# Layer 1's gate behind each tile's norm, and gate chunks of 256 columns

## The chip, the cores and the metric

The kernel is one program on one core of a Trainium2 chip. Five engines work side by side, each through its own queue of instructions in a fixed order: TensorE (PE, matrix products), VectorE (DVE), ScalarE (ACT), GpSimd (POOL) and SyncE (SP), which here only issues DMAs. The metric is the device time of one execution in microseconds (us); the kernel before takes 2372.92 us, the median of three runs from 2371.53 to 2376.02.

## The reference

A decoder trunk of two layers over 1024 tokens of width 1024, all in float32. Layer 0 (retention and mLSTM heads) isn't touched by the change. Layer 1, cut to what matters:

```
u    = rmsnorm(h, norm_pre)
proj = u @ cd_w_in                      # q, k, v, gates, z (1024 wide) and the S5 part
y    = [nsa(...) * silu(z) | s5(...) * silu(sz)] @ cd_w_out       # (1024+512) -> 1024
h    = h + rmsnorm(y, norm_post)
h    = h + sigmoid(h @ pe_gate) * (p @ pe_proj)                   # the gate stage; this is the output
```

`nsa` is attention of 16 heads in 4 groups, with compressed, selected and sliding-window keys.

## The kernel before

Each float32 operand of a product is split into a high and a low part (names end in h and l, or hi and lo), and a product is three products of parts: high by high, high by low, low by high. A product of a 128-token tile with 512 output columns over 1024 inputs is 8 x 3 = 24 PE instructions of 512 columns, over 256 inputs 2 x 3 = 6.

Layer 1 runs in three stages. First come the projections (`nsa_projections`, a generator whose steps are called one by one). Its last part makes z in 16 steps, from weights that `chunk` loads and splits: 2 chunks of 512 columns, 4 load steps each, every one in a buffer of the pool `wsp` (6 of high, 6 of low parts). The same pool then holds the keys and values of a head group, which `group` loads (names kh, kl, vt).

Second comes the attention: 32 units, 4 groups by 8 token tiles, of which one is worked at a time: scores (PE `sc`), softmax (DVE, ACT), scaling of the probabilities `pr` (partly on POOL), their transposes (PE `pt`, split into `pthh` and `pthl`), products with the values (PE `av`). The first PE instruction of a unit's end is `av<-cp,vcT`, by which units are counted here. Beside the units runs a generator, `filler`, that carries other work in small steps; `step` calls it after each part of a unit, so many times as `share` gives for the group. The steps in order: the S5 branch's GLU (PE `gl`), its part of the output product (`fp`, stored to yD), the p products `p @ pe_proj` (stored to ppD), the output products of groups 0, 1 and then 2 (added in yD), and last, for each token tile of group 3 in the order `LAST`, the group's output product, the norm and the residual (lines 1580 to 1605), which leave h in DRAM (hD[2]). The filler has one PSUM buffer (`pF`), four buffers of 512 columns for loaded tiles (tag fin) and four for results (tag fo).

Third, after the attention, `gate_stage` runs the whole gate of layer 1, 8 tiles by 2 halves by 24 products (PE `gp`), with 8 PSUM buffers: it loads h and the stored p products and stores the output. One tile's norm (the last unit's, `late_tile`) is done there too.

The order of the instructions on each engine is made by a scheduler when the program is built, from priorities (`FOFF` sets the filler behind the attention) and buffers; on the chip it is fixed. SP issues its DMAs in that order, and a DMA whose data or buffer isn't ready holds up all behind it.

Of the kernel before, what the change touches and what calls it, by code (L numbers as in the profile page):

```python
# [25 lines left out]
S = 1024  # L26
# [71 lines left out]
def body(tc, A, out, dbg=None):  # L98
# [980 lines left out]
    def nsa_projections(pd):  # L1079
# [47 lines left out]
        for c in range(2):  # L1127
            ck = chunk(W1, [(2608 + 512 * c, 512)])
            for half in range(2):
                for m in range(4):  # L1130
                    ps = pz[0][0].tile([128, 512], FT, name="pj", tag=pz[0][1])
                    proj_col(ps, uT, half, ck, m * 128)
                    zt = pd[0].tile([128, 2, 512], FT, name="zt", tag="st")[:, 0]
                    s.activation(zt, ps, AF.Tanh, scale=0.5)
                    v.scalar_tensor_tensor(zt, zt, 1.0, ps, op0=OP.add, op1=OP.mult)
                    nc.sync.dma_start(zD[4 * c + m, :, half * 512:(half + 1) * 512], zt)
                    yield
# [19 lines left out]
    with ExitStack() as e:  # L1157
# [307 lines left out]
    ext1 = Ext(dict(x=xf), "xxwxwwxw")  # L1465
    with ExitStack() as e:
# [24 lines left out]
        def filler():  # L1491
# [8 lines left out]
            def local_parts(x, nk, eng):  # L1500
                hi = pf.tile([128, 4, 256], FR, name="fhi", tag="fhi")[:, :, :128]
                lo = pf.tile([128, 4, 256], FR, name="flo", tag="flo")[:, :, :128]
# [18 lines left out]
            for l0 in range(0, 8, 2):  # L1521
                hi = pf.tile([128, 4, 256], FR, name="fhi", tag="fhi")
                lo = pf.tile([128, 4, 256], FR, name="flo", tag="flo")
# [22 lines left out]
            for src, w, kt0, nk, dst, add in ((None, W2, 8, 4, yD, False),  # L1546
                                              (A["p"][1, 0], A["pe_proj"][1], 0, 2, ppD, False),
                                              (mixN, W2, 0, 4, yD, True),
                                              (mixN, W2, 4, 2, yD, True)):
                wq = weights(w, kt0, nk)  # L1550
                for i in range(NT):
                    while src is mixN and not all((q, i) in ready for q in ((0, 1) if kt0 == 0 else (2,))):
                        yield
# [14 lines left out]
                    for hf in range(2):  # L1568
                        hs = slice(hf * 512, (hf + 1) * 512)
                        y = ftile("fy", "fo")  # L1570
                        s.activation(y, product(T, wq[hf], nk), AF.Copy, scale=0.25 if src is None else 1.0)
# [6 lines left out]
            wq = wlast[0] = [[load_w(W2, [(hf * 512, 512)], 6, 2)] for hf in range(2)]  # L1578
            for i in LAST[:-NL]:
                while (3, i) not in ready:  # L1580
                    yield
                rows = slice(i * 128, (i + 1) * 128)
                hv = [slice(hf * 512, (hf + 1) * 512) for hf in range(2)]
                x = ready[3, i]
# [3 lines left out]
                T = local_parts(x, 2, g)  # L1588
# [8 lines left out]
                for hf in range(2):  # L1597
# [9 lines left out]
        wlast = [None]  # L1607
# [3 lines left out]
        share = {0: 30, 1: 26, 2: 20, 3: 64}  # L1611
        ready = {}

        def step(gg, n):
            credit[0] += share[gg] * n / 66
            while credit[0] > 0.99:
                credit[0] -= 1
                with tc.issue_after(pace[0].ins), tc.high_priority(offset=FOFF):
                    next(fill, None)

        FOFF = -1000
        for n, (gg, i) in enumerate(units):
            rows = slice(i * 128, (i + 1) * 128)
            zt = n2.tile([128, 2, 128], FT, name="zn", tag="zn", bufs=3)
# [32 lines left out]
            if gg < 3 or i in LAST[-NL:]:  # L1657
# [5 lines left out]
    qx_ = ExitStack()  # L1663
    psB = qx_.enter_context(tc.tile_pool(name="psB2", bufs=5, space=PSUM, reuse_waits="tile"))
    psA = qx_.enter_context(tc.tile_pool(name="psA2", bufs=3, space=PSUM, reuse_waits="tile"))
    with ExitStack() as e:
        pw = e.enter_context(tc.tile_pool(name="pw4", bufs=1, reuse_waits="tile"))

        def late_tile(i, y):

            rows = slice(i * 128, (i + 1) * 128)
            x = pw.tile([128, 2, 128], FT, name="lx", tag="lx")
            nc.sync.dma_start(x, mixN[6:8, :, rows].rearrange("a p k -> p a k"))
            nc.sync.dma_start(y, yD[rows, :])
            x2 = pw.tile([128, D], FT, name="lr", tag="lr")
            gp = pw.tile([128, D], FT, name="lg", tag="lg")
            nc.sync.dma_start(gp, row_ap(A["norm_post"][1], D))
            T = pw.tile([128, 2, 8, 128], FR, name="mhl", tag="thl", bufs=4)[:, :, :2]
            T = T[:, 0], T[:, 1]
            halve(*T, x)  # L1680
            for hf in range(2):
                hs = slice(hf * 512, (hf + 1) * 512)
                ps = psA.tile([128, 512], FT, name="op", tag="psA")
                proj_tok(ps, local(*T), i, wlast[0][hf], 512, nkt=2)
                v.tensor_tensor(y[:, hs], y[:, hs], ps, op=OP.add)
            ms = sm.tile([128, 1], FT, name="ms", tag="ms")
            s.activation(x2, y, AF.Square, accum_out=ms)
            nc.sync.dma_start(x2, hD[1][rows, :])
            r = rstd_of(ms, 1, 1.0 / D, "rs")
            v.scalar_tensor_tensor(y, y, r, gp, op0=OP.mult, op1=OP.mult)  # L1690
            v.tensor_tensor(y, y, x2, op=OP.add)
# [3 lines left out]
    qx_.close()  # L1695
# [33 lines left out]
```

## Time and profile before

The profiled execution took 2375.35 us, with a span of 2373.5 us from the first to the last instruction, so 1.9 us lie outside; it is 2.4 us above the median.

| stretch, us | what runs | PE busy us | DVE | POOL | PE clock |
|---|---|---|---|---|---|
| 1588.29 to 1733.30 | attention group 0, units 2 to 8 | 138.13 | 114.84 | 65.78 | 0.96 |
| 1733.30 to 1908.40 | group 1 | 169.77 | 144.16 | 65.01 | 0.98 |
| 1908.40 to 2087.20 | group 2 | 166.44 | 157.46 | 90.37 | 0.98 |
| 2087.20 to 2237.76 | group 3, units 25 to 31 | 139.25 | 130.95 | 100.81 | 0.95 |
| 2237.76 to 2260.00 | end of unit 32 | 13.26 | 16.13 | 15.24 | 0.92 |
| 2260.00 to 2373.50 | gate stage | 101.80 | 36.02 | 5.19 | 0.97 |

A stretch begins at the first `av` product of a unit. Up to 1500 us PE is busy nearly all the time. Busy time of PE counts a product that runs at half clock twice as long, so a full row isn't PE at its peak.

### The profile page before, as it was taken

To read this page: it belongs to the slowest core of one execution; us is meant where nothing else is said; L and a number is where in the kernel's file an instruction comes from. 1 tells how busy PE (TensorE), PEld (TensorE's weight loads), DVE (VectorE), ACT (ScalarE), POOL (GpSimd) and SP (SyncE) were. 2 spreads that over 40 slices of the span, in tenths; PEclk is the share of its full clock that TensorE was granted. 3 is DMA by queue.
4 is the path that set the end of the run, shared out by engine and by line. 5 is a ranking of instruction groups with operands and counts; after the bars stand their busy time and mean duration, and the time that the engine had idled before them with its cause. 6 is when DMAs were issued, how large, how long until landed. Compare 5 with 4: busy or idle time off the path is not lost.

```text
span 2373.5 us, 34461 instructions
## 1 busy us (share of the span) xinstructions
PE 2279.9 (96%) x11974; PEld 1906.6 (80%) x11974; DVE 1465.5 (62%) x3877; ACT 1069.6 (45%) x2329; POOL 487.5 (21%) x585
## 2 busy tenths in 40 slices
PE   7999999999999999999999999989999989999888
PEld 6878789788888788888888898778888768787667
DVE  6777747755554434343487333377777898898833
ACT  6233323433332432233332332266777777688721
POOL 0122200000000000200000000044544244566710
PEclk9999999999999999999999999989999999999999
DMA  6323312021221745314477423262453333355443
GB/s 159 91 80 104 101 45 72 27 72 35 64 72 36 239 147 203 136 69 134 127 224 234 113 72 116 87 166 67 123 161 117 118 113 101 115 171 162 164 159 112
DMA packets 264647, 279.26 MB, mean 118 GB/s; under 512 B 54384, under 2 KB 196312, under 8 KB 264442
## 3 DMA queue, kind: packets, MB, share of 16 engines
q1 hardware_dynamic: 252618, 243.95, 33.2%
q10 hardware_dynamic: 8240, 24.20, 3.0%
q0 software_dynamic: 3616, 8.92, 1.3%
q8 instruction: 95, 1.56, 0.3%
q14 instruction: 78, 0.64, 0.1%
HBM read 189.84 MB, written 88.42 MB: 117 GB/s over the span
## 4 chain that ended last, share of the span: by engine, by line
PE 82%; DVE 7%; DMA 6%; issue 2%; SPq 2%; ACT 1%; POOL 1%; ACTq 0%; DVEq 0%; POOLq 0%
PE pj L139 40%; PE gp L139 7%; PE op L139 6%; PE fp L139 5%; PE av L139 4%; PE sc L139 4%; PE pt L1485 4%; PE yp L139 2%; PE gl L139 2%; DVE pr L1425 1%; PE trp L214 1%; PE cs L139 1%; PE pp L139 1%; DVE pthl L1477 1%; PE hp L139 1%
## 5 line engine op out<-in xcount | busy, mean ns | idle before, releaser
L139 PE MATMUL pj<-whi,uh 128*128 128x512 f32 (+2 forms) x768 | 278.1, 363 | 4.6 <-ACT whi L163 3.1
L139 PE MATMUL pj<-whi,ul 128*128 128x512 f32 (+2 forms) x768 | 277.4, 361 | 0.0
L139 PE MATMUL pj<-wlo,uh 128*128 128x512 f32 (+2 forms) x768 | 277.3, 361 | 0.0
L1428 ACT ACTIVATE pr<-pr,nm 128x640 f32<-128x640 f32 (+7 forms) x256 | 187.4, 733 | 67.1 <-DVE nm L1425 62.7
L139 PE MATMUL pj<-vh,whi 128*128 128x512 f32 x512 | 204.5, 400 | 0.2 <-ACT vh L218 0.2
L139 PE MATMUL pj<-vh,wlo 128*128 128x512 f32 x512 | 201.9, 394 | 0.0
L139 PE MATMUL pj<-vl,whi 128*128 128x512 f32 x512 | 201.9, 394 | 0.0
L164 DVE SCALAR_TENSOR_TENSOR wlo<-raw,gnp,whi 128x512 fp32r<-128x512 f32 (+3 forms) x248 | 142.5, 611 | 75.4 <-ACT whi L163 74.3
L1477 DVE TENSOR_TENSOR pthl<-pt,pthh 128x512 fp32r<-128x512 f32 x264 | 176.4, 683 | 20.0 <-ACT pthh L1476 16.4
L1476 ACT ACTIVATE pthh<-pt 128x512 fp32r<-128x512 f32 x264 | 149.2, 592 | 49.2 <-PE pt L1485 43.6
L163 ACT ACTIVATE whi<-raw,gnp 128x512 fp32r<-128x512 f32 (+3 forms) x248 | 134.9, 605 | 78.9 <-PE pj L139 36.2
L139 PE MATMUL op<-whi,mhl 128*128 128x512 f32 x520 | 165.1, 395 | 2.5 <-ACT mhl L218 1.7
L139 PEld LDWEIGHTS pj<-whi,uh 128*128 128x128 f32 x768 | 145.0, 189 | 27.6 <-ACT whi L163 3.3
L1485 PE MATMUL pt<-consts,pr 128*128 128x128 f32 x1056 | 162.4, 280 | 4.2 <-DVE pr L1442 2.0
L139 PEld LDWEIGHTS pj<-wlo,uh 128*128 128x128 f32 x768 | 145.7, 190 | 22.3 <-issue 0.7
L139 PEld LDWEIGHTS pj<-whi,ul 128*128 128x128 f32 x768 | 144.8, 189 | 22.1 <-issue 0.2
L1485 PEld LDWEIGHTS pt<-consts,pr 128*128 128x128 f32 x1056 | 133.0, 144 | 28.2 <-issue 4.6
L139 PE MATMUL gp<-whi,mhl 128*128 128x512 f32 x480 | 154.8, 398 | 0.0
L139 PE MATMUL sc<-kh,q 128*128 128x320 f32 (+5 forms) x384 | 142.2, 373 | 11.2 <-DVE nm L1425 10.3
L1442 POOL TENSOR_SCALAR pr<-pr,cf 128x640 f32<-128x640 f32 (+4 forms) x64 | 114.7, 1793 | 150.1 <-DVE cf L1437 71.0
L139 PE MATMUL av<-pthl,vt 128*128 128x512 f32 x264 | 117.5, 445 | 15.8 <-DVE pthl L1477 15.2
L139 PE MATMUL sc<-kl,q 82*128 82x320 f32 (+5 forms) x384 | 127.3, 333 | 0.0
(444 smaller groups left out, 5549.3 us busy)
## 6 DMA issues: line engine op xcount, KB each, us to landing
raw<-in_ab_w_in_dram SPq DMA_DIRECT2D x100, 256.0 KB
raw<-in_cd_w_in_dram SPq DMA_DIRECT2D x30, 512.0 KB
yD<-fy SPq DMA_DIRECT2D x48, 256.0 KB
raw<-in_ab_w_out_dram SPq DMA_DIRECT2D x16, 512.0 KB
raw<-in_pe_gate_dram SPq DMA_DIRECT2D x16, 512.0 KB
qD<-qst SPq DMA_DIRECT2D x16, 512.0 KB
q<-qD SPq DMA_DIRECT2D x32, 256.0 KB
fin<-yD SPq DMA_DIRECT2D x32, 256.0 KB
```

The source lines that it names most:

```text
L139: return t.matmul(o, l, r, start=start, stop=stop, **k)
L163: s.activation(hi[:, k], raw[:, k], AF.Copy, scale=gain(kt0 + k))
L164: v.scalar_tensor_tensor(lo[:, k], raw[:, k], gain(kt0 + k), hi[:, k].bitcast(FT), op0=OP.mult, op1=OP.subtract)
L214: t.transpose(ps[:, k * 128:(k + 1) * 128], x[:, (k4 + k) * 128:(k4 + k + 1) * 128], ident)
L1425: v.tensor_tensor_reduce(pr[:, x:y], ps[:, :y - x], mask[:, x:y], op0=OP.add, op1=OP.min, scale=-1.0, scalar=nm[:, 0:1] if c else 3e38, ac ...
L1428: s.activation(pr[:, :nk], pr[:, :nk], AF.Exp, scale=-1.0, bias=nm[:, c:c + 1], accum_out=sums[:, b, h:h + 1])
L1442: (v if eng == "v" else g).tensor_scalar(P[h][:, :nk], P[h][:, :nk], cf[:, h:h + 1], None, op0=OP.mult)
L1476: s.activation(hi[:dst_shape], ps[:dst_shape], AF.Copy)
L1477: v.tensor_tensor(lo[:dst_shape], ps[:dst_shape], hi[:dst_shape].bitcast(FT), op=OP.subtract)
L1485: t.transpose(ps[:, h * 128:(h + 1) * 128], P[h][:, k * 128:(k + 1) * 128], ident)
```

## The change

Three things are changed. The z weights come in 4 chunks of 256 columns, two load steps each (4 row blocks a step), and the keys of group 0 are asked for one step later (11 for 10). The p products stand behind the output products of groups 0 and 1, and the shares of the four groups are 22, 18, 22 and 76 for 30, 26, 20 and 64. And `gate_stage` is no longer called for layer 1: the filler's last part is, for each of the 8 tiles, `normed` (output product of group 3 and the norm, as before, now with h kept in the two buffers y[0] and y[1]), `turned` (h transposed and split, and both parts stored to a DRAM tile gT) and `gated_out` for the first 512 columns, in the order: norm of a tile, gate of the tile before it, transposes of the tile. The second 512 columns of seven tiles are a generator of their own, `rest`, which loads the transposed parts (gh, gl) and the second half of h (gr) again and uses the attention's buffers; it is run in turn with what is left of the filler after the last unit. The last tile does both halves itself. Where such tiles follow each other, y[0] takes two of the four buffers of tag fo in turn, y[1] one and the gate's `th` one.

```diff
@@ nsa_projections
-        for c in range(2):
-            ck = chunk(W1, [(2608 + 512 * c, 512)])
+        for c in range(4):
+            ck = chunk(W1, [(2608 + 256 * c, 256)])
             for half in range(2):
-                for m in range(4):
+                for m in range(2):
...
-            if n == 10:
+            if n == 11:
                 KV = {0: group(0)}
@@ filler
             for src, w, kt0, nk, dst, add in ((None, W2, 8, 4, yD, False),
+                                              (mixN, W2, 0, 4, yD, True),
                                               (A["p"][1, 0], A["pe_proj"][1], 0, 2, ppD, False),
-                                              (mixN, W2, 0, 4, yD, True),
                                               (mixN, W2, 4, 2, yD, True)):
...
+            gw[0] = [load_w(Wg, [(0, 512)], 2 * k, 2, wp=xf) for k in range(4)]
+            gw[1] = [load_w(Wg, [(512, 512)], 0, 2)]
+            def normed(i):
...
-                    g.tensor_tensor(y[hf], y[hf], x, op=OP.add)
-                    nc.sync.dma_start(hD[2][rows, hv[hf]], y[hf])
+                    (v if done else g).tensor_tensor(y[hf], y[hf], x, op=OP.add)
+                nc.sync.dma_start(hD[2][rows, hv[1]], y[1])
                 yield
+                return y
+            def turned(i, y):
+                hi, lo = (pf.tile([128, 4, 256], FR, name=n, tag=n, bufs=2).rearrange("p a (b k) -> p (a b) k", k=128)
+                          for n in ("fhi", "flo"))
+                for hf in range(2):
+                    ps = pF.tile([128, 512], FT, name="ft", tag="pf")
+                    for k in range(4):
+                        t.transpose(ps[:, k * 128:(k + 1) * 128], y[hf][:, k * 128:(k + 1) * 128], ident)
...
+                    s.activation(hi[:, ks], p3_, AF.Copy)
+                    v.tensor_tensor(lo[:, ks], p3_, hi[:, ks].bitcast(FT), op=OP.subtract)
+                    yield
+                for a, x in enumerate((hi, lo)):
+                    nc.sync.dma_start(gT[i, :, a, :], x.bitcast(FT).rearrange("p k n -> p (k n)"))
...
+            for i in LAST:
...
+                y = yield from truly(normed(i))
+                yield from truly(gate)
+                T = yield from truly(turned(i, y))
+                gate = gated_out(i, 0, T, y[0], pF, "pf")
+            yield from truly(gate)
+            yield from truly(gated_out(i, 1, T, y[1], pF, "pf"))
...
+        def gated_out(i, hf, T, h, pool_, tag):
+            rows, hs = slice(i * 128, (i + 1) * 128), slice(hf * 512, (hf + 1) * 512)
+            ps = pool_.tile([128, 512], FT, name="gp", tag=tag)
+            for k in range(0, 8, 4):
+                proj_tok(ps, local(*(x[:, k:k + 4] for x in T)), 0, gw[hf][k // 2:], 512, nkt=4, start=k == 0, stop=k == 4)
+                yield
+            pp = pf.tile([128, 512], FT, name="pp", tag="fin", bufs=4)
+            nc.sync.dma_start(pp, ppD[rows, hs])
+            th = pf.tile([128, 512], FT, name="th", tag="fo", bufs=4)
+            s.activation(th, ps, AF.Tanh, scale=0.5)
+            v.scalar_tensor_tensor(th, th, 1.0, pp, op0=OP.add, op1=OP.mult)
+            (v if done else g).tensor_tensor(th, th, h, op=OP.add)
+            nc.sync.dma_start(dst_[rows, hs], th)
+        def rest():
+            def fetch(i):
...
+                for a in range(2):
+                    nc.sync.dma_start(T[a].rearrange("p k n -> p (k n)").bitcast(FT), gT[i, :, a, :])
+                nc.sync.dma_start(h, hD[2][i * 128:(i + 1) * 128, 512:])
...
+                yield from gated_out(i, 1, T, h, pS, "sc")
...
-        share = {0: 30, 1: 26, 2: 20, 3: 64}
+        share = {0: 22, 1: 18, 2: 22, 3: 76}
...
-        for _ in fill:
-            pass
+        gw[1] += [load_w(Wg, [(512, 512)], 2 * k, 2) for k in range(1, 4)]
+        done.append(True)
+        gens = [fill, rest()]
+        while gens:
+            for x in list(gens):
+                if x in gens and next(x, gens) is gens:
+                    gens = [y for y in gens if y is not x]
...
-        gate_stage(pw, 1, ext1, hD[2], out if out is not None else dbg["o"], ppD=ppD, order=[7, 6, 5, 0, 1, 2, 4, 3],
-                   late={i: late_tile for i in LAST[-NL:]})
```

What the scheduler makes of it is shown at three places. The first is ACT's queue in the tail, behind the last unit. Before, it holds `mhl<-trp` (the reading of the transposed h), and `th<-gp` (the tanh that ends each half's 24 gate products), freely mixed:

```order
L218 ACTIVATE mhl<-trp 128x512 x2
L963 ACTIVATE th_23734<-gp 128x512
L218 ACTIVATE mhl<-trp 128x512 x2
L963 ACTIVATE th_23765<-gp 128x512
L963 ACTIVATE th_23796<-gp 128x512
L963 ACTIVATE th_23828<-gp 128x512
L218 ACTIVATE mhl<-trp 128x512
L470 ACTIVATE mhl<-lx 128x256
L218 ACTIVATE mhl<-trp 128x512
L963 ACTIVATE th_23927<-gp 128x512
```

In the changed kernel, `fhi<-ft` is the reading of a transposed half (`turned`), `fhi<-zn` the split of a unit's result for its output product, `fin,ms<-fy` the square and sum of the norm, and `fy<-fy,rsb` its scaling (`normed`):

```order
L1657 ACTIVATE th<-gp 128x512
L1616 ACTIVATE fhi<-ft 128x512
L1496 ACTIVATE fhi<-zn 128x2x128
L1616 ACTIVATE fhi<-ft 128x512
L1593 ACTIVATE fin,ms_23240<-fy 128x512 x2
L1601 ACTIVATE fy<-fy,rsb 128x512 x2
L1657 ACTIVATE th<-gp 128x512
L1616 ACTIVATE fhi<-ft 128x512
L1496 ACTIVATE fhi<-zn 128x2x128
L1616 ACTIVATE fhi<-ft 128x512
L1593 ACTIVATE fin,ms_23495<-fy 128x512 x2
L1601 ACTIVATE fy<-fy,rsb 128x512 x2
```

Each tile's five rows come in the same order, with one `th<-gp` (the first 512 columns) to a tile; no gate product of the second 512 columns ends in this piece. PE's queue is alike: 24 `gp`, 8 `ft`, 12 `fp` for a tile. All 384 gate products of the layer stand in PE's queue behind the first `av` product of unit 32, in both kernels.

The second place is SP's queue in the same stretch, with what each row waits for (DMAHWn is the landing of an earlier DMA on one of eight lanes that the program uses in turn, the engines' names are work done there). Before, it loads h and the p products and stores the output:

```order
L967 DMA out_dram<-h_23513 128x1024 [waits DMAHW0_49,DVE_49]
L934 DMA h_23833<-hD_98 128x1024 [waits DMAHW1_49,DMAHW0_49,PE_49]
L961 DMA pp<-ppD 128x512 [waits DMAHW4_49,DVE_49]
L961 DMA pp<-ppD 128x512 [waits DMAHW7_49,DVE_49]
L961 DMA pp<-ppD 128x512 [waits DMAHW2_49,DVE_49]
L967 DMA out_dram<-h_23530 128x1024 [waits DVE_49]
L1674 DMA h_23850<-yD 128x1024 [waits DMAHW6_49,DMAHW5_49,PE_49]
```

In the changed kernel, for one tile: the store of the transposed low part, the loads of both transposed parts, the norm's gain and the residual for both halves, the p products, the store of h's second half, and the next tile's y from yD:

```order
L1620 DMA gT<-flo 128x1024 [waits DMAHW6_49,DVE_49]
L1668 DMA gh<-gT 128x1024 [waits DMAHW7_49,DMAHW5_49]
L1668 DMA gl<-gT 128x1024 [waits DMAHW6_49]
L1599 DMA fin<-in_norm_post_dram 128x512 [waits DMAHW1_49]
L1600 DMA fin<-hD_97 128x512 [waits DMAHW2_49]
L1599 DMA fin<-in_norm_post_dram 128x512 [waits DMAHW3_49,Activation_49]
L1600 DMA fin<-hD_97 128x512 [waits DMAHW4_49,Activation_49]
L1655 DMA pp<-ppD 128x512 [waits DMAHW1_49,Pool_49]
L1604 DMA hD_98<-fy 128x512 [waits Pool_49]
L1587 DMA fy<-yD 128x512 [waits DMAHW7_49,Pool_49]
L1660 DMA out_dram<-th 128x512 [waits DMAHW0_49]
L1587 DMA fy<-yD 128x512 [waits DMAHW6_49,PE_49]
```

The loads of gh and gl have come in ahead of the norm's loads, and each waits for the landing of the gT store that it reads; the second load of fy, into the only buffer of y[1], waits for the store of hD in the row above the first.

The third place is SP's queue where the projections end and the attention begins (`zD<-zt` stores a z step; kh, kl and vt are keys and values). Before:

```order
L1153 DMA vt<-vD 128x8x128 x2
L1146 DMA kh<-kD 64x1024
L1147 DMA kh<-kD 64x1024
L1148 DMA kl<-kD 64x1024
L1149 DMA kl<-akD 18x1024
L1146 DMA kh<-kD 64x1024
L1147 DMA kh<-kD 64x1024
L1148 DMA kl<-kD 64x1024
L1136 DMA zD<-zt 128x512
L1149 DMA kl<-akD 18x1024
```

In the changed kernel the values of group 0 stand ahead of the last five stores of z, and the last store of z stands behind the first loads of the filler:

```order
L1353 DMA q_14182<-qD 128x4x128
L1354 DMA q_14183<-qD 64x4x128
L1355 DMA q_14183<-aqD 18x4x128
L1146 DMA kh<-kD 64x1024
L1147 DMA kh<-kD 64x1024
L1148 DMA kl<-kD 64x1024
L1149 DMA kl<-akD 18x1024
L1153 DMA vt<-vD 128x8x128 x2
L1525 DMA fin<-y5D 128x4x128 x2
L1136 DMA zD<-zt 128x512
```

## Rows read from the trace of the kernel before

**Rows 1.** the page: PE's busy time, and the chain that ended last by engine.

```profile
PE 2279.9 (96%) x11974; PEld 1906.6 (80%) x11974; DVE 1465.5 (62%) x3877; ACT 1069.6 (45%) x2329; POOL 487.5 (21%) x585
PE 82%; DVE 7%; DMA 6%; issue 2%; SPq 2%; ACT 1%; POOL 1%; ACTq 0%; DVEq 0%; POOLq 0%
```

**Rows 2.** by stretch: busy us (instructions) of PE, PEld, DVE, ACT, POOL; clock, DMA share, GB/s.

```profile
1733.30:1908.40 175.10, 169.77 (x954) 143.97 (x953) 144.16 (x457) 136.04 (x299) 65.01 (x69) 0.98 0.38 122
1908.40:2087.20 178.80, 166.44 (x902) 134.56 (x900) 157.46 (x449) 132.97 (x271) 90.37 (x88) 0.98 0.34 107
2087.20:2237.76 150.56, 139.25 (x749) 113.57 (x747) 130.95 (x387) 123.31 (x282) 100.81 (x99) 0.95 0.54 172
2260.00:2373.50 113.50, 101.80 (x460) 82.19 (x460) 36.02 (x54) 19.28 (x35) 5.19 (x5) 0.97 0.37 132
```

**Rows 3.** timeline of PE: first product of units 28 and 32.

```profile
2167.68 0.39 PE L139 MATMUL av<-cp,vcT 128*128 128x512 f32 x1
2237.76 0.40 PE L139 MATMUL av<-cp,vcT 128*128 128x512 f32 x1
```

**Rows 4.** chain of waits, 2180 to the end: start us, us, what.

```profile
2199.94 5.07 DMA hD<-fy
2205.03 2.11 DMA fy<-yD
2218.36 3.54 DMA fy<-yD
2230.68 5.37 DMA hD<-fy
2236.07 2.58 DMA fy<-yD
2254.89 4.58 DMA fin<-in_norm_post_dram
2266.17 6.36 DMA h<-hD
2345.23 22.44 PE gp L139 x96
```

**Rows 5.** instructions of a normed tile, by line: duration ns min/median/max.

```profile
L1592 DVE TENSOR_TENSOR fy<-fy,fp x14: 667/682/690, 2169.4 to 2254.0; 128x512 f32<-128x512 f32 x14
L1593 ACT ACTIVATE fin<-fy x14: 619/626/644, 2170.1 to 2254.8; 128x512 f32<-128x512 f32 x14
L1593 ACT ACTIVATION_READ_ACCUMULATOR fin<-fy x14: 186/193/210, 2170.6 to 2255.3; 128x1 f32 x14
L226 POOL TENSOR_TENSOR rsb<-rsa,mhalf x8: 548/566/731, 2176.3 to 2328.9; 128x1 f32<-128x1 f32 x8
L1601 ACT ACTIVATE fy<-fy,rsb x14: 707/710/728, 2178.7 to 2257.9; 128x512 f32<-128x512 f32 x14
L1602 POOL TENSOR_TENSOR fy<-fy,fin x14: 1260/1288/1301, 2179.5 to 2262.2; 128x512 f32<-128x512 f32 x14
```

**Rows 6.** page, costliest groups: reading a 128x512 PSUM tile into two parts.

```profile
L1477 DVE TENSOR_TENSOR pthl<-pt,pthh 128x512 fp32r<-128x512 f32 x264 | 176.4, 683 | 20.0 <-ACT pthh L1476 16.4
L1476 ACT ACTIVATE pthh<-pt 128x512 fp32r<-128x512 f32 x264 | 149.2, 592 | 49.2 <-PE pt L1485 43.6
```

**Rows 7.** timeline of the last microseconds: ACT and SP.

```profile
2367.69 0.60 ACT L963 ACTIVATE th<-gp 128x512 f32<-128x512 f32 x1 [5.01 <-PE gp L139]
2369.77 0.34 SPq L967 DMA_DIRECT2D out_dram<-h  x1
```

**Rows 8.** timeline around the first attention unit: PE, SP, DVE.

```profile
1537.75 1.36 PE L1485 MATMUL pt<-consts,pr 128*128 128x128 f32 x11
1554.15 0.35 SPq L1136 DMA_DIRECT2D zD<-zt  x1
1561.16 1.89 DVE L1477 TENSOR_TENSOR pthl<-pt,pthh 128x512 fp32r<-128x512 f32 x3 [2.41 <-DMA vt<-vD]
1561.91 0.80 PE L139 MATMUL av<-pthl,vt 128*128 128x512 f32 x1 [5.80 <-DVE pthl L1477]
```

More of the change, by code (lines that the diff above doesn't have):

```diff
@@ L1464, in body @@
     W2 = A["cd_w_out"][0]
-    ext1 = Ext(dict(x=xf), "xxwxwwxw")
     with ExitStack() as e:
@@ L1577, in filler @@
                         yield
[L1578 to L1581, printed above, removed]
+            wq = [[load_w(W2, [(hf * 512, 512)], 6, 2)] for hf in range(2)]
+            gw[0] = [load_w(Wg, [(0, 512)], 2 * k, 2, wp=xf) for k in range(4)]
+            gw[1] = [load_w(Wg, [(512, 512)], 0, 2)]
+            def normed(i):
                 rows = slice(i * 128, (i + 1) * 128)
                 hv = [slice(hf * 512, (hf + 1) * 512) for hf in range(2)]
-                x = ready[3, i]
                 y = [ftile("fy", "fo") for _ in range(2)]
@@ new lines, in filler @@
+            gate = iter(())
+            for i in LAST:
+                while (3, i) not in ready:
+                    if next(gate, False) is False:
+                        yield False
+                    else:
+                        yield True
+                y = yield from truly(normed(i))
[4 more added lines that the diff above has]
+            yield from truly(gated_out(i, 1, T, y[1], pF, "pf"))
@@ new lines, in truly @@
+        def truly(gen):
+            while True:
+                try:
+                    next(gen)
+                except StopIteration as e:
+                    return e.value
+                yield True
+        def gated_out(i, hf, T, h, pool_, tag):
[11 more added lines that the diff above has]
+            nc.sync.dma_start(dst_[rows, hs], th)
@@ new lines, in rest @@
+        def rest():
+            def fetch(i):
+                T = [np_.tile([128, 1024], FR, name="g" + x, tag="pr0", bufs=5).rearrange("p (k n) -> p k n", k=8) for x in "hl"]
+                h = np_.tile([128, 640], FT, name="gr", tag="pr1", bufs=4)[:, :512]
+                for a in range(2):
+                    nc.sync.dma_start(T[a].rearrange("p k n -> p (k n)").bitcast(FT), gT[i, :, a, :])
+                nc.sync.dma_start(h, hD[2][i * 128:(i + 1) * 128, 512:])
+                return T, h
+            X = {}
+            for n, i in enumerate(LAST[:-1]):
+                for m in (n, n + 1):
+                    if m not in X and m < len(LAST) - 1 and LAST[m] in stored:
+                        X[m] = fetch(LAST[m])
+                while n not in X:
+                    yield
+                    if i in stored:
+                        X[n] = fetch(i)
+                T, h = X[n]
+                yield from gated_out(i, 1, T, h, pS, "sc")
@@ L1608, in body @@
+        Wg, dst_ = A["pe_gate"][1], out if out is not None else dbg["o"]
+        gT = dram.tile([8, 128, 2, S], FT, name="gT")
+        gw, done, stored = {}, [], set()
         fill = filler()
         credit = [0.0]
-        share = {0: 30, 1: 26, 2: 20, 3: 64}
+        share = {0: 22, 1: 18, 2: 22, 3: 76}
         ready = {}
@@ L1616, in step @@
             while credit[0] > 0.99:
+                with tc.issue_after(pace[0].ins), tc.high_priority(offset=FOFF):
+                    work = next(fill, None)
+                if work is False:
+                    break
                 credit[0] -= 1
-                with tc.issue_after(pace[0].ins), tc.high_priority(offset=FOFF):
-                    next(fill, None)
         FOFF = -1000
```

53 lines of the change are left out of this document (14 added, 39 removed).

## The prediction

> **What bounds the kernel now.** I read the page first: PE is busy for 96% of the span and holds 82% of the chain that ended last [rows 1], so time can only come from where PE waits or runs at half clock. The stretches say where. In group 1 PE is busy for 169.77 of 175.10 us, so filler work taken out there is time gained. In group 3 it is 139.25 of 150.56 at a mean clock of 0.95, with DVE at 130.95 and POOL at 100.81: something else ends waits there [rows 2]. Units 28 to 31 take 2237.76 - 2167.68 = 70.1 us [rows 3], while PE's queue holds for them 66 filler products, 44 products with values, 70 of scores (at most 512 columns each), 84 transposes and 16 short ones. At 22.44 / 96 = 0.234 us for a product of 512 columns [rows 4], 1.36 / 11 = 0.12 us for a transpose [rows 8] and an estimated 0.2 for a score, that is 25.7 + 14 + 10 + 2 = 52 us. So about 18 us are waits or half clock, and the chain shows what kind: between 2200 and 2240 it runs through the filler's own DMAs, h stored, then the next y loaded, 7.2 to 8 us for each such pair [rows 4]. Last, the tail. From the start of unit 32 to the end is 2373.5 - 2237.76 = 135.7 us, and the gate stage keeps PE busy for 101.80 of its 113.50 us [rows 2].
>
> **The change part by part.** The z chunks: PE's products stay the same, the load steps too (8), but 32 splits of 256 columns replace 16 of 512 on ACT and on DVE. A half-width split costs no more than a whole one, so 16 extra at no more than 0.6 to 0.7 us [rows 6] are at most 11 us on each engine, beside a stretch of some 100 us that PE fills. I put it at nothing; were PE to wait for weights there, it is those 11 us. Where the attention begins, PE waits 5.8 us until 1561.91, for a DVE instruction that was let go at 1561.16; its buffer is free only when the last z store has landed, and that store left SP at 1554.15 [rows 8]. In the new queue the values of group 0 go five z stores earlier, and SP isn't held by them before the last store; but kh, kl and vt of group 1 and two loads of y5D still stand ahead. Gain between 0 and 7 us; I take 3, the middle.
>
> The filler: behind unit 32's start PE's queue holds 72 fp products for 24 before (12 of them named op), so units 1 to 31 hold 48 fewer, 11.2 us of PE. By groups it is +10, -34, -24 and 0. The loss is in groups 1 and 2, where PE is busy for 97% and 93%, so nearly all of it should show: 9 us, with 3 to 11 as bounds, less where a unit is then bound by DVE. In group 3 norm tiles leave (five tiles' output products and norms, or more, now lie behind unit 32) and p products come, which need no POOL and end in one ACT read. Of the 18 us of waits in units 28 to 31 I take 5 back; the bounds are 0 and 12. Together the last unit begins 17 us earlier (3 to 30).
>
> The tail. The gate isn't hidden in the attention: all 384 of its products stand behind unit 32's start, as before. Behind that point PE has 72 + 384 + 21 = 477 products and 72 transposes, 111.6 + 8.6 = 120 us at full clock, against 429 and 92, 100.4 + 11 = 111 us, that took 135.7. So PE has 9 us more to do, and what decides is how long it waits. Before, eight PSUM buffers and loads made well ahead kept it fed. Now the order for tiles 5, 0, 1, 2 is 24 gp, 8 ft, 12 fp, again and again, with no product of the second half between, as ACT's queue shows (one tanh to a tile); and all three kinds use the one buffer of pF. One cycle, from the DVE add that ends a tile's output product to the next tile's, goes so:
> - square and its sum 0.63 + 0.19, two tiny DVE operations (estimate 0.3), power 0.57, scaling 0.71: 2.4 us; then POOL, two products and two sums of 1.29 each: 5.15 [rows 5]. h is ready after 7.6 us.
> - its second half is stored, and the next y[1] loads into the same buffer only when that has landed: 5.07 to 5.37 us from store to load, then 2.11 to 3.54 until y is there [rows 4], and 0.68 for the add [rows 5]. That closes the cycle at 15.5 to 17.2 us.
> - PE's own work in it is 36 products and 8 transposes, 8.4 + 1.0 = 9.4 us, with two reads of 0.59 + 0.68 [rows 6] behind the transposes. These fit beside the chain. PE waits 6 us or more in each.
> - The norm's gain and residual are late too. SP sends them behind gh and gl, and these wait until the gT store has landed. A 512 KB store that left at 2369.77 with nothing beside it took the 3.7 us to the end of the span [rows 7]. The y load leaves 3.3 us before the new cycle begins and the stores right behind it, so gh and gl leave at about +1 and the gain at +2 to +3; with 1 MB ahead of it (512 KB took 6.36 us, a gain of 256 KB 4.58 [rows 4]) it lands at +5.5 to +8.5, where POOL wants it at +2.4. That adds 3 to 6 us: 19 to 23.
>
> I take 20 us a cycle. To the end of tile 5's output product there are 83 products and 24 transposes, 22.3 us, and some reads: 25. Four cycles are 80. Behind them stand 207 products and 16 transposes (48.4 + 1.9), now with second halves between, and the last tile's reads: 56. The end, tanh to landed store, was 5.8 [rows 7] and is 5 with half the store. 25 + 80 + 56 + 5 = 166, 30 more than 135.7. With cycles of 16 us it is 150, 14 more; with 25, 186, 50 more.
>
> Sum: -17 + 30 = +13. The profiled execution's own 2375.35 us (span plus 1.9) becomes 2388; the median of the runs lies 2.4 lower, so I forecast 2386.
>
> On what a DMA takes: the rows show 5.07 and 5.37 us for a store of 256 KB and 2.11 to 3.54 for a load [rows 4]. The Trainium skill (DMA: Bandwidth & Descriptors, section Anatomy of one DMA) gives about 2.0 us fixed plus the bytes at 436 GB/s, an estimate of 2.6 us for either. Loads agree with that, stores don't. By it a cycle would be near 14 us and the time near the first rival's.
>
> **The rivals.** First, faster: the queue is calm once the attention has ended, every DMA lands in the 2.11 us of the shortest row [rows 4] and the gain is in time. Then a cycle is 7.6 + 2.1 + 0.4 + 2.1 + 0.7 = 13 us, the tail 25 + 52 + 56 + 5 = 138, and the time 2372.9 - 17 + 2.3 = 2358. For it: the attention's loads are gone. Against: a cycle moves 4.5 MB (gT out and back 2, y, gain and residual 1.5, p, h and output 1), in 13 us 346 GB/s, twice the 172 of group 3 [rows 2]. The point is the cycle: below 15.5 us the kernel is faster, from 15.5 to 17.9 it can't be told from no change, above it is slower.
>
> Second, no change: cycles of 16 to 17 us, that is no lateness of the gain but slow stores. 25 + 66 + 56 + 5 = 152, +16, and 2372.
>
> Third, much slower: the 4.5 MB crowd the queue so that stores and gain land later still, 25 us a cycle, and groups 1 and 2 give back little because DVE (157.46 of 178.80 in group 2 [rows 2]) takes over: -10 + 50, 2413. Half of it, no gain in the attention (-3) with cycles of 20, is 2400.
>
> **How the numbers follow.** Forecast, slower by cycles of 18 to 22 us: 0.50, with its own range 2378 to 2400. Much slower: 0.18. No change: 0.13. Faster: 0.19. About 0.2%, 4.7 us, can be told from no change here. So slower 0.68, same 0.13, faster 0.19. The range that leaves a tenth on either side is 2362 to 2412: it takes in half of the first rival's case and most of the third's.
>
> **What would show it.** In the profile after, unit 32's first value product should stand near 2221 us (2208 to 2235), and about 166 us should follow it. In that stretch PE should be busy for about 0.75 of the time, with four cycles in which 24 gp, 8 ft and 12 fp take 18 to 22 us, and a clock below 0.95 there. PE's waits should be for DVE's add of the output product, which waits for fy<-yD, and for POOL's sums behind fin<-in_norm_post. The second halves should run together at the end at 0.234 us a product. PE should wait less than 5.8 us where the attention begins. The forecast is wrong if the cycles take under 16 us, if the second halves' products fill them, or if the attention ends more than 30 us earlier.

## The result, and the profile after

The changed kernel is slower: 2429.24 us (median of four runs, 2425.1 to 2432.67), a ratio of 1.0232 to the kernel before, interval 1.0207 to 1.0257, or +55 us. The forecast was 2386, with 2412 as the upper end: right in sign, and too small by more than its range allowed. The kernel before took between 2365.6 and 2374.5 us (medians) beside the change and the runs below, so kernels are compared by their ratios.

By its page PE is busy for 2298.5 us, for 2279.9 before [rows 1], in a span that is 50 us longer. The stretches say where the time is. Unit 32 begins at 2222.57, 15.2 us earlier than [rows 3]. These are groups 1, 2 and 3 and then everything from unit 32 on, which I call the tail (columns as in [rows 2]):

```profile
1723.62:1885.89 162.27, 158.57 (x894) 132.44 (x892) 138.98 (x427) 126.17 (x271) 73.05 (x75) 0.99 0.39 119
1885.89:2067.59 181.70, 168.15 (x902) 136.31 (x900) 157.43 (x474) 134.81 (x280) 79.04 (x81) 0.95 0.31 97
2067.59:2222.57 154.98, 140.20 (x761) 114.16 (x760) 128.50 (x374) 121.98 (x273) 82.49 (x77) 0.95 0.45 147
2222.57:2423.30 200.73, 146.11 (x550) 108.75 (x548) 51.96 (x83) 43.80 (x86) 45.40 (x43) 0.83 0.55 182
```

The tail of the kernel before, the same view:

```profile
2237.76:2373.50 135.74, 115.06 (x522) 92.02 (x520) 52.14 (x80) 33.84 (x65) 20.43 (x17) 0.96 0.39 138
```

The tail is 65.0 us longer. PE is idle in it for 200.73 - 146.11 = 54.6 us (before 20.7) and busy for 31 us more; 9 of those are the added work that the prediction counted (120 against 111 us at full clock), the other 22 are, as an estimate, more products at the lower clock level (0.83 of the full clock for 0.96). The prediction divided the tail into three parts: up to tile 5's output product, four tile cycles, the rest. It gave them 25, 80 and 61 us; they took 26.5, 89.5 and 84.7:

```profile
2222.57:2249.06 26.49, 23.54 (x107) 18.37 (x106) 10.29 (x17) 10.39 (x20) 8.37 (x8) 0.96 0.59 185
2249.06:2338.59 89.53, 65.64 (x222) 47.07 (x221) 17.44 (x29) 20.11 (x41) 30.12 (x28) 0.77 0.57 191
2338.59:2423.30 84.71, 56.93 (x224) 43.31 (x222) 24.22 (x37) 13.30 (x25) 6.90 (x7) 0.85 0.52 171
```

In a cycle one link of the forecast's chain is the main one: the gT store has to land before SP sends the loads behind it, the norm's gain among them, and only then can POOL start (start, us, what):

```profile
2266.80 5.49 DMA gT<-flo
2272.30 0.32 SPq L1668
...
2272.67 6.46 DMA fin<-in_norm_post_dram
...
2279.27 1.26 POOL fy L1602
...
2281.87 2.49 POOL fy L1603 x2
...
2284.99 1.26 POOL th L1659
2286.26 0.69 POOL flo L1497
...
2288.81 5.60 DMA gT<-flo
```

From one gT store to the next that is 2288.81 - 2266.80 = 22.0 us. The other link of the forecast, the store of h and the load of y behind it, isn't on this chain: in the four cycles DVE's adds of an output product waited for PE's product (3.0 to 3.1 us in most) or not at all, never for y. PE has a chain of its own of the same length through its one buffer: the first gate product of a tile starts at 2274.06, of the next at 2295.41. In between PE waits for the readings of pF and once for POOL's sum (in brackets), and its products follow each other at 0.43 us, but for the second 12 gate products, which take 0.23:

```profile
2274.06 0.79 PE L139 MATMUL gp<-whi,fhi 128*128 128x512 f32 x1 [0.78 <-DVE fy L1592]
...
2275.07 0.63 PE L139 MATMUL gp<-whi,flo 128*128 128x512 f32 x1
2275.50 0.63 PE L139 MATMUL gp<-whi,fhi 128*128 128x512 f32 x1
...
2279.46 0.40 PE L139 MATMUL gp<-wlo,fhi 128*128 128x512 f32 x1
2279.69 0.39 PE L139 MATMUL gp<-whi,flo 128*128 128x512 f32 x1
...
2283.19 0.66 PE L1614 MATMUL ft<-consts,fy 128*128 128x128 f32 x4 [1.06 <-POOL fy L1603]
2285.66 0.87 PE L1614 MATMUL ft<-consts,fy 128*128 128x128 f32 x4 [1.81 <-DVE flo L1617]
2287.94 0.80 PE L139 MATMUL fp<-whi,fhi 128*128 128x512 f32 x1 [1.41 <-DVE flo L1617]
...
2291.70 0.79 PE L139 MATMUL fp<-whi,fhi 128*128 128x512 f32 x1 [0.83 <-DVE fy L1592]
...
2295.41 0.79 PE L139 MATMUL gp<-whi,fhi 128*128 128x512 f32 x1 [0.78 <-DVE fy L1592]
```

The rest is where the forecast had no waits. The two longest of PE there:

```profile
2354.19 0.80 PE L139 MATMUL gp<-whi,gh 128*128 128x512 f32 x1 [9.08 <-ACT th L1657]
...
2398.27 1.12 PE L1614 MATMUL ft<-consts,fy 128*128 128x128 f32 x4 [7.42 <-ACT th L1657]
```

And the chain up to the first of them:

```profile
2339.47 4.99 DMA fin<-in_norm_post_dram
2344.60 1.28 POOL fy L1602
2345.89 3.38 DMA pp<-ppD
2349.29 0.70 DVE th L1658
...
2350.74 2.72 DMA out_dram<-th
2353.54 0.61 ACT th L1657
2354.19 7.39 PE gp L139 x24
```

PE waits for a tanh to read a full PSUM buffer; the tanh for the store of the half before it, since th has one buffer; that half for its p products, whose load needs one of the four buffers fin, which the norm's gain and residual fill too: SP sends it at 2345.89, when POOL's product with the gain has ended. In the whole tail ACT stands idle for 31.3 us, six times, until such a store has landed.

### The profile page after: what moved, and what is told of

It is laid out like the page before. It is cut to its first block, busy times and chain, and to the rows that moved or that the text cites. A ratio compares the mean times of both kernels' runs of the same rounds, so it can differ in the third digit from the quotient of the medians.

```text
span 2423.3 us, 34597 instructions
## 1 busy us (share of the span) xinstructions
PE 2298.5 (95%) x11974; PEld 1912.2 (79%) x11974; DVE 1466.9 (61%) x3890; ACT 1076.1 (44%) x2349; POOL 494.6 (20%) x591
## 5 line engine op out<-in xcount | busy, mean ns | idle before, releaser
L164 DVE SCALAR_TENSOR_TENSOR wlo<-raw,gnp,whi 128x256 fp32r<-128x256 f32 (+3 forms) x264 | 144.8, 587 | 75.8 <-ACT whi L163 74.9
L1476 DVE TENSOR_TENSOR pthl<-pt,pthh 128x512 fp32r<-128x512 f32 x264 | 176.1, 683 | 20.1 <-ACT pthh L1475 17.3
L163 ACT ACTIVATE whi<-raw,gnp 128x256 fp32r<-128x256 f32 (+3 forms) x264 | 138.0, 586 | 79.7 <-PE pj L139 38.3
L139 PE MATMUL av<-pthh,vt 128*128 128x512 f32 x264 | 111.3, 422 | 7.9 <-ACT pthh L1475 7.9
```

The costliest lines, as they stand in the source:

```text
L139: return t.matmul(o, l, r, start=start, stop=stop, **k)
L163: s.activation(hi[:, k], raw[:, k], AF.Copy, scale=gain(kt0 + k))
L164: v.scalar_tensor_tensor(lo[:, k], raw[:, k], gain(kt0 + k), hi[:, k].bitcast(FT), op0=OP.mult, op1=OP.subtract)
L1476: v.tensor_tensor(lo[:dst_shape], ps[:dst_shape], hi[:dst_shape].bitcast(FT), op=OP.subtract)
```

## The experiments

In the table, "unit 32" and "tail" are from each kernel's profiled run (us), the ratio is to the kernel before on the same chip.

| run | unit 32 at | tail | median us | ratio (95%) |
|---|---|---|---|---|
| e1 z256 | 2220.7 | 135.2 | 2360.76 | 0.9964 (0.9949 to 0.998) |
| e2 z256_porder | 2235.1 | 163.4 | 2397.18 | 1.0117 (1.0082 to 1.0151) |
| e3 th_buffers | 2219.5 | 197.1 | 2421.37 | 1.0224 (1.0196 to 1.0252) |
| e4 gain_kept | 2222.0 | 194.3 | 2427.14 | 1.0247 (1.021 to 1.0283) |
| e5 tail_psum | 2223.7 | 175.9 | 2400.5 | 1.0139 (1.0114 to 1.0165) |
| e6 p_first | 2235.7 | 176.0 | 2417.18 | 1.0229 (1.0194 to 1.0263) |
| e7 porder_old_shares | 2247.4 | 132.0 | 2385.58 | 1.0087 (1.0055 to 1.0119) |
| e8 p_first_psum_th | 2241.2 | 158.1 | 2400.17 | 1.0141 (1.0121 to 1.0162) |
| e9 hold | 2220.1 | 205.0 | 2430.2 | 1.0251 (1.0228 to 1.0273) |
| e10 hold_busy | 2223.4 | 208.8 | 2432.6 | 1.0263 (1.0239 to 1.0288) |
| e11 hold_psum_th | 2219.8 | 175.9 | 2399.23 | 1.0117 (1.0087 to 1.0147) |
| e12 hold_gain | 2218.2 | 159.8 | 2383.81 | 1.006 (1.0038 to 1.0082) |
| e13 direct | 2227.6 | 149.9 | 2373.27 | 1.002 (1.0007 to 1.0034) |
| e14 direct_gain | 2216.8 | 143.7 | 2365.15 | 0.9988 (0.9971 to 1.0006) |
| e15 direct_p_first | 2234.6 | 132.8 | 2373.86 | 1.0012 (0.9995 to 1.0029) |

**Which part of the change costs what: e1, e2, e7, e6.** e1 is the kernel before with the first hunk of the diff alone.

> The kernel before with the z chunks of 256 columns (and the keys of group 0 asked for a step later) alone. The changed kernel's first attention unit ended 8.5 us earlier by then (second unit's first value product at 1579.82 for 1588.29). If the chunks did that: the second unit at about 1580 and a time 6 to 9 us below the kernel before, 2365. Rival: the lighter filler of group 0 (share 22 for 30) did it: the second unit at about 1587, time within 3 us of before.

It is faster, ratio 0.9964, -8.5 us. The wait of 5.80 us [rows 8] is gone, but PE now waits 7.51 us for the step before it, where it waited 3.25 before (in the changed kernel, second piece, 7.76). The second unit starts at 1580.47 for 1588.29:

```profile
1556.75 0.80 PE L139 MATMUL av<-pthh,vt 128*128 128x512 f32 x1 [7.51 <-ACT pthh L1476]
...
1580.47 0.39 PE L139 MATMUL av<-cp,vcT 128*128 128x512 f32 x1
```

```profile
1558.26 0.80 PE L139 MATMUL av<-pthh,vt 128*128 128x512 f32 x1 [7.76 <-ACT pthh L1475]
```

Unit 32 comes 17.0 us earlier, with all other parts of the change left out; in this run groups 0 and 3 were 5.6 and 3.0 us shorter too. By the ratio half of that, 8.5 us, is gained; the rest lies between the two profiled runs. e2 adds the new order of the p products and the new shares, e7 the order alone, both on the kernel with the old gate stage. Both also take over the changed kernel's `step`, in which a call that finds the filler blocked no longer uses up credit, so that the order is never tested without it.

> The kernel before with the z chunks, the p products behind the output products of groups 0 and 1, and the shares 22, 18, 22, 76; its own gate stage stays. If what the change gained in the attention is a gain by itself: the last unit's first value product some 10 to 20 us earlier than 2237.76, and a time of 2355 to 2366. Rival: filler moved out of groups 1 and 2 comes back in group 3 and behind it, so that only the z chunks' 8 us are left or less: 2364 to 2375.

> The kernel before with the z chunks and the p products moved, but with its own shares 30, 26, 20, 64. If it was the shares that cost the 36 us of e2 (less filler in groups 0 to 2, so more norm tiles late): 2358 to 2370. If it was the order of the products: 2390 to 2400.

e2 came out above both of its ranges, e7 (by its ratio 2394) in its second. Against e1, e2 is 1.5% slower and e7 1.2%, so most of the loss is the order's. In e7 the tail is no longer than that of e1 and group 1 is the main loser (first row): 198 us for 173.4, with x1032 on PE for x957. By the code the filler, blocked until the outputs of groups 0 and 1 are there, keeps its credit and then works in a burst; group 2 has those products less and got only 6 us shorter, and group 3 8 us longer. With the smaller shares (e2) most of the loss comes out behind unit 32 instead (second row, x564 for x522 in e1): some 30 more products of output products stand there, with their norms, ahead of the gate stage.

```profile
1719.93:1917.89 197.96, 190.49 (x1032) 160.95 (x1032) 145.62 (x439) 138.38 (x294) 93.07 (x90) 0.98 0.42 131
```

```profile
2235.07:2398.50 163.43, 129.39 (x564) 101.62 (x562) 58.56 (x97) 44.59 (x87) 37.56 (x32) 0.91 0.45 148
```

e6 goes the other way: the changed kernel with the p products first and the old shares.

```diff
+                                              (A["p"][1, 0], A["pe_proj"][1], 0, 2, ppD, False),
                                               (mixN, W2, 0, 4, yD, True),
-                                              (A["p"][1, 0], A["pe_proj"][1], 0, 2, ppD, False),
...
-        share = {0: 22, 1: 18, 2: 22, 3: 76}
+        share = {0: 30, 1: 26, 2: 20, 3: 64}
```

> The changed kernel with the p products in front of the output products again and the shares 30, 26, 20, 64, as before the change; z chunks and gate in the filler stay. The p order alone cost some 36 us beside the z chunks in the kernel with the old gate stage (e2 against e1). If it costs as much here (norm tiles pushed behind the last unit): 2385 to 2400, that is what the gate in the filler costs alone, with the last unit at about 2221 and a tail of 165 to 180. If the tail's length is the gate cycles' alone, whatever stands ahead: 2415 to 2430.

Its ratio is 1.0229, that of the change, as in the second expectation: unit 32 is 13 us later, the tail 25 us shorter, in the profile; in the runs' ratio nothing. So beside the new gate the order and the shares cost nothing that the runs can tell, and the price of the gate in the filler is e6 against e1: 1.0229 / 0.9964, +2.7% or 63 us. The parts don't add up: beside the new order and shares the gate costs 1.0232 / 1.0117, some 27 us, and the order with its shares costs 36 beside the old gate (e2 against e1).

**Single causes in the tail: e3, e4, e5, e8.** e3 gives th three buffers, e4 loads the gain once, e5 spreads the tail over the attention's free PSUM buffers:

```diff
-            th = pf.tile([128, 512], FT, name="th", tag="fo", bufs=4)
+            th = (n2.tile([128, 512], FR, name="th", tag="pthh", bufs=3).bitcast(FT) if done else
+                  pf.tile([128, 512], FT, name="th", tag="fo", bufs=4))
```

```diff
...
-                gate = gated_out(i, 0, T, y[0], pF, "pf")
+                gate = gated_out(i, 0, T, y[0], *((pT, "pt") if done else (pF, "pf")))
...
```

> The changed kernel, but the gate's result th behind the attention takes three buffers of its own (those of the probabilities' high parts, free by then), which also leaves all four result buffers to the two halves of the normed tile. Theory A (the tail is long since a tanh waits until the store of the half before it has landed, and PE behind the tanh): the 31 us that ACT stood idle for these landings go, the waits of 9.08 and 7.42 us on PE go, and the second halves' products run within the tile cycles: 2400 to 2410 for 2429. Theory B (the tail is long since SP sends the norm's gain and residual behind the loads of gh and gl, which wait for the gT store): the cycles stay at 21 us, 2420 to 2428.

> The changed kernel, but the norm's gain is loaded once behind the attention, into a buffer of the mask that is free by then, for 2 loads of 256 KB in each tile. Theory B (the gain, queued behind gh, gl and the gT store, comes late to POOL): four cycles shrink from 21 us by 3 to 5, 2409 to 2418. Theory A (result buffers): the residual still stands in the same place of SP's queue and the end of the tail is as it was, 2422 to 2430.

> The changed kernel, but behind the attention the gate's first halves and the transposes take the attention's free PSUM buffers (three of pT) and the second half of an output product that of pV, for the one buffer of pF. Theory C (a tile's cycle of 21.3 us is PE's own chain through one PSUM buffer, each step waiting for the reading of the one before, and that at half the clock since PE has gaps): the waits of PE for th, flo and fy at 0.8 to 1.8 us each go, the cycles fall to 15 to 17 us and the granted clock in the tail rises above 0.81: 2400 to 2412 for 2429. Theory D (the cycle is DVE, POOL and the y load): the cycles stay at 20 to 21 us, PE waits for POOL's or DVE's fy instead: 2422 to 2430.

e3 and e4 changed the ratio by no more than its interval. e5 took some 22 us off (1.0139 for 1.0232). All three had a flaw that I saw only then: "if done" is decided when the code of a tile is written out, and the tiles of the first cycles are written out while units are still left. So e4 is no test of theory B (e12 is): of the 12 loads of the gain in the changed kernel's tail 8 are still there, those of the cycles.

In e3 the edit did reach the second halves. The waits of 9.08 and 7.42 us for a tanh are gone and some second halves stand in the cycles, as theory A has it, but the tail is only 3.6 us shorter: PE now waits 5.28 and 6.52 us for DVE, whose reading of pF (flo) stands in its queue behind the halves' own products with p:

```profile
2359.35 1.12 PE L1614 MATMUL ft<-consts,fy 128*128 128x128 f32 x4 [5.28 <-DVE flo L1617]
...
2394.57 1.12 PE L1614 MATMUL ft<-consts,fy 128*128 128x128 f32 x4 [6.52 <-DVE flo L1617]
```

In e5 the first cycles keep the one buffer and are much as they were: between gate starts 20.2, 23.9 and 20.3 us for 21.4, 21.2 and 22.8. Its gain is in the part behind them, the third of the prediction: from the fifth gate start to the end it takes 60.9 us, in the changed kernel 83.9 (the rows of both, e5 first), and no wait of PE for a tanh above 0.8 us is left.

```profile
2338.75:2399.60 60.85, 51.45 (x221) 40.71 (x219) 22.97 (x34) 11.54 (x22) 7.11 (x6) 0.95 0.67 226
```

```profile
2339.37:2423.30 83.93, 56.23 (x220) 43.09 (x220) 23.54 (x36) 13.28 (x25) 6.90 (x7) 0.85 0.52 172
```

e8 is e6 with the edits of e3 and e5.

> The changed kernel with p products first and the old shares, with the tail's PSUM buffers of pT and pV and with three th buffers. If p order, PSUM buffer and th buffer add up (36, about 20 and 8 us): 2360 to 2375, level with the kernel before. If the norm chain and its DMAs bound the tail whatever the buffers: 2385 to 2400.

1.0141, 0.9% below e6: as much as the PSUM buffers alone brought in e5. The parts don't add up.

**All tiles alike: e9 to e11.** e9 writes six of the tiles out behind the attention, in turn with the second halves:

```diff
-                while (3, i) not in ready:
+                while (3, i) not in ready or i in LAST[2:] and not done:
```

> The changed kernel, but the filler takes up only the first two tiles of group 3 while units are left; the other six are written out behind the attention, in turn with the second halves. Nothing else is changed, and PE's queue then has 24 products of a second half in every tile cycle, where the changed kernel has four cycles without. Theory E (the second halves stand at the end because the tiles were written out ahead of them, and the cycles without them run at half clock with gaps): cycles of 60 products and 8 transposes, 15 us at full clock, take 18 to 20 us, nothing is left for the end, the tail falls from 200.7 to 150 to 165 us and the granted clock rises above 0.9: 2380 to 2395 for 2429. Theory F (each cycle is the chain of y load, norm and PSUM reads, whatever PE has beside it): cycles of 24 to 28 us, 2410 to 2430.

Theory E falls. Now each cycle has 60 products, but takes 25 to 27 us, after a first of 32. The idle time of PE in this tail, by what it waited for (us in total, times, longest):

```profile
PE ft L1614 <- DVE flo L1617: 10.7, 7, 2.9
PE ft L1614 <- ACT th L1657: 10.1, 5, 4.1
PE gp L139 <- DMA gh<-gT: 8.9, 4, 3.3
PE gp L139 <- DMA gl<-gT: 7.2, 4, 2.3
PE fp L139 <- DVE flo L1617: 7.1, 5, 1.4
```

No wait is the main one. The second half of a tile, moved into the cycles, now waits for its own round trip through gT.

> e9 with products added that nobody reads: 6 behind the transposes of a half, 3 behind a half's output product, 18 to a tile in six tiles, some 108 products or 25 us at full clock, put where PE waits for pF to be read. If PE's gaps cost through the clock: the clock in the tail rises, and the time is at most 5 us above e9 or below it. If the clock is no matter (PE is bound by its work or by the chain): 15 to 25 us above e9.

```profile
2223.43:2432.20 208.77, 163.92 (x658) 126.83 (x656) 58.90 (x94) 43.86 (x86) 33.50 (x32) 0.89 0.51 174
```

108 products that nobody reads (x658 for x550) cost 3.7 us in the tail and nothing that the runs can tell, at a clock of 0.89 for 0.86. PE's work isn't what bounds the cycles. Whether the clock alone costs anything can't be told from this: PE was busy for 20 us more and little else moved.

> e9 with the tail's PSUM buffers of pT and pV and three th buffers, now for all six tiles (in e5 and e3 the first four cycles, written out before, kept the one buffer). If the waits for the one pF buffer (0.8 to 1.8 us, six to a cycle) are what is left: the cycles fall to 16 us and the tail to 135 to 145, 2365 to 2378. If the norm's loads and stores bound it: no more than 5 us below e9.

1.0117: 31 us below e9, between its two expectations, and still 22 to 23 us a cycle. PE's waits for pF are gone; the chain of DMAs is left, here from one gT store to the next:

```profile
2336.29 3.42 DMA gT<-fhi
...
2341.09 6.03 DMA fin<-in_norm_post_dram
...
2347.25 1.27 POOL fy L1603
...
2349.29 1.12 PE ft L1616 x4
2350.41 7.07 PE gp L139 x22
...
2359.12 3.24 DMA gT<-fhi
```

**The DMA chain: e12 to e15.** e12 is e11 with the gain loaded once; e13 is e11 with the second halves made from the parts where they lie; e14 is both; e15 is e14 with the p products first. From the diff of e13:

```diff
...
-                nc.sync.dma_start(hD[2][rows, hv[1]], y[1])
+                if i in LAST[:2]:
+                    nc.sync.dma_start(hD[2][rows, hv[1]], y[1])
...
+                if i in LAST[2:]:
+                    gate = both(gate, gated_out(i, 1, T, y[1], pT, "pt"))
...
```

> e11 with the norm's gain loaded once behind the attention. In e11 a tile's cycle is still 22 us, and the chain of waits runs through the gT store (3.0 to 3.4 us), then the gain load sent behind it (5.7 to 6.0), POOL's product, the transposes, 22 gate products and the next gT store. If the gain's place in SP's queue holds the cycle: it falls by 4 to 6 us in five cycles, 2370 to 2380 for 2399. If the residual's load, which stands in the same place, takes over: within 4 us of e11.

> e11 without the round trip through DRAM for the last six tiles: their second halves take the transposed parts and h from the buffers in which they were made, so that gT and h aren't stored and gh, gl, gr not loaded (2.5 MB less for a tile); the gain is loaded for each tile as before. If the round trip (the store's landing and SP's queue behind it) holds the cycle: 16 to 17 us, PE's own 14 and a little, the tail 135 to 145: 2360 to 2370. If the order of norm, turn and gate holds it in itself: 20 us and more, 2385 to 2400.

> e13 and e12 together: no round trip and the gain loaded once, three PSUM buffers, three th buffers. Six tiles of 60 products and 8 transposes are 15 us each at full clock. If DMA was all that held the cycles: the tail is that of e1 (135), and the time that of e1 or a few us above (2360 to 2368), since units 2 to 31 take as long. If it stays above 2375 the norm's chain through ACT, POOL and DVE is what is left.

All three went the way of their first theories, e12 and e13 not quite so far. In e11 the gain's place in SP's queue is worth 13 us (1.006 for 1.0117), the round trip 23 (1.002), both 31 (0.9988). In e14's tail PE has the 550 instructions of the changed kernel's, and is busy for 123.63 us for 146.11, the clock at 0.95 for 0.83; the second half of a tile is transposed at 2294.83, 2311.06, 2326.98 and 2343.05, a cycle of 16 us with 60 products in it (first row and the two pieces of the timeline). The second row is e1's tail: PE is idle for 20.1 us in both, so what e14's tail is longer by, 8.5 us, is PE's added work, not waiting.

```profile
2216.82:2360.50 143.68, 123.63 (x550) 97.52 (x548) 61.85 (x94) 43.22 (x86) 33.82 (x32) 0.95 0.41 136
```

```profile
2220.74:2355.90 135.16, 115.05 (x522) 91.91 (x520) 51.89 (x80) 33.54 (x65) 20.12 (x17) 0.95 0.40 139
```

```profile
2294.83 0.63 PE L1620 MATMUL ft<-consts,fy 128*128 128x128 f32 x4 [0.57 <-DVE fy L1607]
...
2311.06 0.63 PE L1620 MATMUL ft<-consts,fy 128*128 128x128 f32 x4 [0.58 <-DVE fy L1607]
```

> e14 with the p products in front and the shares 30, 26, 20, 64 again. In e6 that moved the last unit 13 us later and made the tail 25 us shorter, at cycles of 21 us. If with short cycles a tile costs in the tail what it costs in the attention, nothing is gained: 2362 to 2372. If the tail still has waits that the attention would hide: 2350 to 2360, below e1.

1.0012: unit 32 is 18 us later, the tail 11 us shorter, and nothing is gained, nearer to the first expectation. No form of the gate in the filler came below e1, which is the version that beats both kernels.

## Why the prediction was wrong

- **The sign** was right, and the mechanism in part: the gate's work stays behind the attention, and there it runs in cycles in which the gain comes late behind the gT store. Of the 43 us that the forecast missed, 34.7 lie in the tail.
- **The attention**: unit 32 was to begin near 2221 and began at 2222.57, by errors that cancel: that is luck. The z chunks were put at -3, with 7 as their most: the second unit began 8.5 us earlier in the changed kernel, and alone (e1) the chunks gave 8.5 us in the time. The wait where the attention begins, to be less than 5.8 us, was 7.76. Groups 1 and 2 were to give 9 and gave 12.8 - 2.9 = 9.9. Group 3 was to give 5 and took 4.4: taking norms out and putting p products in didn't shorten its waits.
- **The cycle** was put at 20 us, from 19 to 23. The two that hold nothing else took 21.35 and 21.15 (gate start to gate start, up to 2316.56), the four together, with 22 and 24 products of a second half in the first and the last, 89.5 for 80. The order of SP's queue was read rightly: the gain takes 6.46 us behind the gT store's 5.49. But the 7.2 to 8.9 us from the store of h to the loaded y, which the sum closes the cycle with, weren't on the chain, and POOL's two other operations in a cycle (th 1.26, flo 0.69) weren't in the sum: that the cycle came near 20 us is partly luck. I also left out that PE would run largely at half clock, so that its own chain through pF is as long; the 22 us more of busy time stand nowhere in the sum, though a clock below 0.95 was expected.
- **The step that failed** is "Behind them stand 207 products and 16 transposes (48.4 + 1.9), now with second halves between, and the last tile's reads: 56". PE was busy for 56.93 us in that part, but it lasted 84.7 with the end. Two thirds of the tail's miss (23.7 of 34.7 us) are there. I costed it as PE's work, and took the halves in between for cover; yet each half's tanh waits for the one th buffer, its store, and a p load that stands behind a norm's loads, and until the tanh has read pF, PE can't go on: waits of the kind that I had priced in the cycles. With more PSUM buffers in just that part (e5) it took 60.9 us from the fifth gate start on, for 83.9 in the changed kernel and 61 in the forecast; with more th buffers alone (e3) the tail got 3.6 us shorter.
- **The rivals**: the first, faster, needed each DMA to land in 2.11 us. On the tail's chain the shortest is 2.56, a store of 256 KB at 2394.96. By the Trainium skill (DMA: Bandwidth & Descriptors, section Anatomy of one DMA — SWDGE (gpsimd) path) a transfer has a fixed cost of about 2 us and then its bytes at 436 GB/s, an estimate of 3.2 us for 512 KB; the section is on DMAs that GpSimd issues, and here SP issues them. The gT stores of 512 KB took 5.49 and 5.60 us in the changed kernel, so the estimate is too short there; in e11 two took 3.42 and 3.24. The third came closest, +50 in the tail, but for another reason: its cycles of 25 us weren't there.
- **The range** ended at 2412 because in the tail the upper case moved only the cycles; the part behind them hangs on the same queue, and erred by more.

## What to carry to other kernels

When work moves behind one queue, price each part of what follows by the chain that feeds it (buffer, store, load), the last part too; a stretch with plenty of PE work isn't covered by it if every piece ends in the same single buffer. A wait that ends last can have another right behind it: taking it away alone then shows nothing (e3). Make sure that an edit reaches the tiles it is meant for (e4 and e5 reached only the last ones), and take the waits away one on top of the other (e11 to e14). And split a change of three parts first: here one part alone was a gain of 0.4%, hidden under a loss of 2.7%, and the other two cost less together than one by one.

## What the runs showed of the hardware

In the four cycles PE was busy for 65.64 of 89.53 us in pieces between waits, and the mean granted clock was 0.77; over the whole tail it was 0.83, and 0.95 in e14, whose tail has as many PE instructions and fewer waits. At the lower level, 1.2 GHz, products of 512 columns followed each other at 0.43 us, at the upper one, 2.4 GHz, at 0.23: in the cycle shown the waits stand before the slow ones, and the fast ones come after gate products without a wait. More products in the gaps (e10) raised the clock from 0.86 to 0.89 and not the speed.

The size of a DMA doesn't tell its time: in the rows above a load of the gain, 256 KB, took from 4.99 to 6.46 us, a gT store of 512 KB from 3.24 to 5.60. What else was in flight then differs too; which part of it made the difference no run shows.
